# Attention scores of two heads next to each other on TensorE, router constants summed on VectorE

## The chip, the cores and the metric

The kernel runs on one core of a Trainium2 chip. The metric is the device time of one execution in microseconds (us). Three runs of the kernel before took 1401.29, 1407.2 and 1399.86 us; their median is 1401.29.

## What is computed

One inference step of two layers for 512 prompt tokens and 8 decode tokens, which share all weights. Layer 0 mixes tokens with a short gated convolution and with differential attention, layer 1 with mLSTM. Each layer ends with layer norm, a hierarchical mixture of 16 experts, a second layer norm and a gated projection. Cut to what the change touches:

```python
# differential attention, layer 0: 8 heads of 64 (4 pairs), prompt in query blocks of 128
s = einsum('bqhd,bkhd->bhqk', q, k) * 64 ** -0.5
s = where(k_pos[None, :] <= q_pos[:, None], s, -inf)
a = softmax(s).reshape(b, 4, 2, tq, tk)
a = a[:, :, 0] - lam * a[:, :, 1]
o = einsum('bhqk,bkhe->bqhe', a, v)
# router of each layer, after the mixer's layer norm with gain g and offset b
x = (z - mean) * rsqrt(var + eps) * g + b
gl = x @ w_group       # (tokens, 4)
el = x @ w_router      # (tokens, 16)
```

## The kernel before

Five engines work side by side: TensorE (PE) multiplies, VectorE (DVE) and ScalarE (ACT) do the elementwise work, GpSimd (POOL) gathers rows by index, and SyncE's queue (SP) starts most transfers. Each engine takes its instructions in order. The kernel is written in a framework whose planner puts the instructions of each engine into their order when the kernel is built: it goes by the order in which the program traces them and by its own estimates of when each could start. `issue_after` keeps chosen instructions of an engine behind a given one.

**Layer 0's input projection** is one loop (`ws_steps`) over 24 blocks of 128 output columns. Weights come in tiles of 1 MB, two blocks each, from SP's queue. Each block is split into a high part (ACT, L137) and a rest (DVE, L138), 128x1024 elements each, and multiplied in three products of 8 steps over two halves of the tokens: 48 matmuls of 256 or 264 columns at L234, accumulated in one of two PSUM tiles `acc`. The next block is split one step ahead. `consume` functions take a finished block out of PSUM: `rope` for queries and keys (ACT copies to `raw`, PE permutes at L396, DVE at L397 to L399), `vcons` for values, and three for the convolution.

**Between the blocks** stands everything else of the mixer, in generators that the loop steps on (`later`, `advance`), one step per block. Constants are made by five small generators at the steps given by `SM`, each held behind the block's matmuls and split by `behind`: the differential weight, the layer norms' constants `lnT`, the convolution's, the router's (L801) and layer 1's. From step 5 on each step also takes one half page set of a decode sequence's keys: a gather of 1 MB on POOL's queue (L455), a product with the query on DVE (L481) and a sum over each head (L482), 16 times.

**Attention** (`attn`, L502 on) works in 16 units, 4 head pairs by 4 query blocks i, added two at a time from step 11 on; two units stand together on PE and are called a cluster. A unit with query block i has nk = 128(i+1) keys. The two heads of a pair lie on partitions 0 to 63 and 64 to 127 of `qT` and `kT`. For each head PE multiplies 64-row tiles into one PSUM tile `tps` of its own (there are four of these tiles, each one bank), and adds the causal mask to the last 128 columns with a bf16 matmul of the identity with the mask. DVE takes the maximum of each head (L516), ACT the exponential (L519), and DVE joins the heads (L524). A step later PE transposes the result (L266), ACT copies it, PE multiplies with the values (L534).

**Router constants.** The router works on layer norms that have not been scaled yet: with w the router's weights (128 partitions, 8 blocks of the model dimension, 20 columns), g and b the norm's gain and offset, it needs g*w, the sum of b*w over the model dimension, and minus the sum of g*w. Before, the sums are matmuls: for each of the two layers 8 matmuls with b as a column spread over 128 columns (L814), then after g*w is formed (L816), in the generator's next step, 8 matmuls with ones (L821). Each is fp32 and runs as two passes on PE, 64 passes in all. The results are copied from PSUM into `c0` (L815, L822).

**What comes behind.** When the blocks and units are done, the output projection's weights are split and multiplied (`mix_all`), decode attention's values are gathered and summed, and the expert weights of layer 0 are loaded through SP into buffers that come free with the mixer (L155). Then follow routing, experts, projection, and all of layer 1.

Of the kernel before, what the change touches and what calls it, by code (L numbers as in the profile page):

```python
# [8 lines left out]
F32 = mybir.dt.float32  # L9
# [5 lines left out]
OP = mybir.AluOpType  # L15
AX = mybir.AxisListType.X
# [34 lines left out]
SM = (1, 3, 4, 5, 7)  # L51
# [69 lines left out]
class K:  # L121
# [233 lines left out]
    def even(self):  # L355
        tc, nc, A, O = self.tc, self.nc, self.A, self.O
        V, S, G, TE = self.V, self.S, self.G, self.T
# [3 lines left out]
        with tc.tile_pool(name="mz", bufs=1) as mz, tc.tile_pool(name="mx", bufs=1) as mx, tc.tile_pool(name="mx2", bufs=2) as mx2:  # L361
            p, p2 = self.mixer_pools()
# [6 lines left out]
            def lambdas():  # L369
                lv = p2.tile([128, 4, 64], F32, name="lv", tag="e")  # L370
                lp = p2.tile([128, 2, 64], F32, name="lp", tag="e")
                for i, n in enumerate(("lambda_q1", "lambda_k1", "lambda_q2", "lambda_k2")):
                    self.bcast(lv[:, i, :], A[n][0], 64)
                self.bcast(sw, A["subln_w"][0], 128)
                yield
                V.tensor_mul(lp, lv[:, 0::2, :], lv[:, 1::2, :])
                V.tensor_reduce(ls[:, 0:2], lp, axis=AX, op=OP.add)
                S.activation(ls[:, 2:4], ls[:, 0:2], AF.Exp)
                V.tensor_sub(ls[:, 4:5], ls[:, 2:3], ls[:, 3:4])
                V.tensor_scalar(ls[:, 5:6], ls[:, 4:5], 0.2, -1.0, op0=OP.add, op1=OP.mult)  # L380
                V.tensor_scalar_mul(sw, sw, 0.8)
# [122 lines left out]
            def attn(hp, i):  # L504
                nk = (i + 1) * 128
                st = p2.tile([128, 8], F32, name="st", bufs=3)
                e = p2.tile([128, 2, 512], F32, name="e")
                pss = []
                for a in range(2):
                    r = slice(64 * a, 64 * a + 64)  # L510
                    ps = self.tp()
                    pss.append(ps)
                    TE.matmul(ps[:, :nk], qT[r, hp, i * 128:i * 128 + 128], kT[r, hp, :nk], start=True, stop=False)
                    TE.matmul(ps[:, i * 128:nk], self.idb, self.cmb, start=False, stop=True)
                for a in range(2):
                    V.tensor_reduce(st[:, a:a + 1], pss[a][:, :nk], axis=AX, op=OP.max)  # L516
                V.tensor_scalar_mul(st[:, 0:2], st[:, 0:2], -0.125)
                for a in range(2):
                    S.activation(e[:, a, :nk], pss[a][:, :nk], AF.Exp, bias=st[:, a:a + 1], scale=0.125,  # L519
                                 accum_out=st[:, 2 + a:3 + a])  # L520
                V.reciprocal(st[:, 4:6], st[:, 2:4])
                V.tensor_mul(st[:, 5:6], st[:, 5:6], nlam)
                S.mul(e[:, 1, :nk], e[:, 1, :nk], st[:, 5:6])
                V.scalar_tensor_tensor(e[:, 0, :nk], e[:, 0, :nk], st[:, 4:5], e[:, 1, :nk], op0=OP.mult, op1=OP.add)  # L524
                yield
                pt_ = self.tp()
                for j in range(i + 1):
                    self.tr_block(pt_[:, j * 128:(j + 1) * 128], e[:, 0, j * 128:(j + 1) * 128], 128)
                aT = mx2.tile([128, 512], F32, name="aT")
                S.copy(aT[:, :nk], pt_[:, :nk])  # L530
                yield
                po = self.tp()
                for j in range(i + 1):
                    TE.matmul(po[:, :128], aT[:, j * 128:(j + 1) * 128], vt[:, j, hp * 128:(hp + 1) * 128],  # L534
                              start=(j == 0), stop=(j == i))
                o = p2.tile([128, 128], F32, name="o")
                S.copy(o, po[:, :128])
                yield from norm_o(o[:, None, :], 128, 1, hp, slice(i * 128, i * 128 + 128))

                if (hp, i) == (3, 0):  # L540
                    ydone.add(1)

            def norm_o(o, n, nh, hp, cols):

                st = mx2.tile([128, 8], F32, name="st2", bufs=3)
                sq = mx2.tile([128, 128], F32, name="sq", bufs=1)
                for h in range(nh):
                    S.activation(sq[:n], o[:n, h, :], AF.Square, accum_out=st[:n, h:h + 1])
                V.tensor_scalar(st[:n, 0:nh], st[:n, 0:nh], 1.0 / 128, EPS, op0=OP.mult, op1=OP.add)
                G.tensor_tensor(st[:n, 4:4 + nh], st[:n, 0:nh], self.c("nhalf")[:n, 0:nh], op=OP.pow)  # L550
                for h in range(nh):
                    V.scalar_tensor_tensor(o[:n, h, :], o[:n, h, :], st[:n, 4 + h:5 + h], sw[:n], op0=OP.mult, op1=OP.mult)
                yield
                ps = self.tp()
                for h in range(nh):
                    self.tr_block(ps[:, h * n:(h + 1) * n], o[:n, h, :], n)
                S.copy(oT[:, hp:hp + nh, cols], ps[:, :nh * n].rearrange("p (h t) -> p h t", h=nh))
# [6 lines left out]
            def conv_consts():  # L564
                sc = p2.tile([19, 512], F32, name="sc", tag="e")
                nc.sync.dma_start(sc[0:16, :], A["state_conv"][0].rearrange("b j f -> (b j) f"))
                nc.sync.dma_start(sc[16:19, :], A["conv_w"][0])
                yield
                ps = self.tp()
                for f in range(4):  # L570
                    self.tr_block(ps[:, f * 19:(f + 1) * 19], sc[:, f * 128:(f + 1) * 128], 19)
                S.copy(scT, ps[:, :76].rearrange("p (f c) -> p f c", f=4))
                G.memset(uT[:, :, 0:2], 0.0)
# [108 lines left out]
            ydone = set()  # L682
            units = [(hp, i) for i in range(4) for hp in range(4)]

            small = dict(zip(SM, (lambdas(), self.norm_consts(p2), conv_consts(), self.router_consts(), self.odd_consts(p2))))
            s = 0
            soft = None
            while True:
# [26 lines left out]
                if s >= USLOT:  # L715
                    for _ in range(min(2, len(units))):
                        self.later(attn(*units.pop(0)))
# [80 lines left out]
            for i in range(2):  # L798
                self.lnT[n, i] = c[:, z, i].rearrange("p g f -> p (g f)")

    def router_consts(self):  # L801

        V, TE, A, cp = self.V, self.T, self.A, self.cp
        w = cp.tile([128, 2, 8, 20], F32, name="wr")
        c0 = cp.tile([128, 2, 2, 20], F32, name="c0")
        for n, c in (("w_group", slice(0, 4)), ("w_router", slice(4, 20))):
            self.nc.sync.dma_start(w[:, :, :, c], A[n].rearrange("i (k p) c -> p i k c", p=128))
        yield
        for i in range(2):
            gT = self.lnT["ln_mix", i]  # L810
            self.wr[i], self.c0[i] = w[:, i], c0[:, i]
            pc = self.tp()
            for k in range(8):
                TE.matmul(pc[:, 0:20], gT[:, 8 + k:9 + k].to_broadcast([128, 128]), w[:, i, k, :], start=(k == 0), stop=(k == 7))  # L814
            V.tensor_copy(c0[:, i, 0], pc[:, 0:20])  # L815
            V.tensor_tensor(w[:, i], w[:, i], gT[:, 0:8, None].to_broadcast([128, 8, 20]), op=OP.mult)  # L816
        yield
        for i in range(2):
            w, pc = self.wr[i], self.tp()
            for k in range(8):  # L820
                TE.matmul(pc[:, 20:40], self.onf, w[:, k, :], start=(k == 0), stop=(k == 7))  # L821
            V.tensor_scalar_mul(c0[:, i, 1], pc[:, 20:40], -1.0)  # L822

    def mix_load(self, i):

# [1219 lines left out]
```

## Time and profile before

| | |
|---|---|
| median of three runs | 1401.29 us (1399.86 to 1407.2) |
| profiled execution | 1403.28 us, span 1401.5 us |
| PE busy | 1293.0 us (92%), 7944 matmuls |
| DVE busy | 857.8 us (61%), 1500 instructions |
| ACT busy | 628.7 us (45%) |
| POOL busy | 250.8 us (18%) |
| DMA | 338.73 MB, mean 242 GB/s |
| granted PE clock, mean | 0.961 |

The span lies between the first and the last instruction of the profiled execution; the execution's own time stands beside it. Busy time counts an engine's instructions and not its waits. Matmuls overlap each other, so a fully busy PE can still be given less to do. An fp32 matmul appears as two instructions, here called passes. [...]

### The profile page before, as it was taken

Reading aid. Unit: us, or ns where it says so; the run is one execution under the profiler, and the core shown is the slowest. Engines: PE = TensorE matmul, PEld = TensorE weight load, DVE = VectorE, ACT = ScalarE, POOL = GpSimd, SP = SyncE. Lnnn points to the kernel's source line nnn. Section 1 sums busy time; section 2 is a strip of 40 time slices with the busy share of each in tenths; the row PEclk is TensorE's granted clock in tenths of the full one; section 3 lists DMA queues with packets and bytes.
Section 4 is the critical chain, followed back from the end, with each engine's and each line's share of the span. In section 5 each row is a group of like instructions: output and inputs, shape, how many; then the busy total and the mean of one; then the engine's idle time right before and its main releaser. Section 6 shows DMA issues by size and latency. Waiting matters only on the chain. (4 is left out here: it accounts for less than half of the span.)

```text
span 1401.5 us, 21016 instructions
## 1 busy us (share of the span) xinstructions
PE 1293.0 (92%) x7944; PEld 987.0 (70%) x7944; DVE 857.8 (61%) x1500; ACT 628.7 (45%) x1053; POOL 250.8 (18%) x242
## 2 busy tenths in 40 slices
PE   8999998996899999997999999999679999988897
PEld 7998876654676655556989988888457565545686
DVE  4689986546985554435745446774698654544472
ACT  3214465122675544436654333332357554444562
POOL 1023222223211121001130000011312221110113
PEclk9989999997799999999999999999879999999999
DMA  7548644893899999999352223384379999999821
GB/s 271 164 159 296 218 141 156 305 350 124 302 324 373 376 301 353 368 334 312 93 158 70 83 65 125 123 306 181 123 279 327 372 356 315 347 376 344 297 63 39
DMA packets 157449, 338.73 MB, mean 242 GB/s; under 512 B 16095, under 2 KB 54459, under 8 KB 153246
## 3 DMA queue, kind: packets, MB, share of 16 engines
q1 hardware_dynamic: 138974, 271.28, 54.3%
q0 software_dynamic: 18224, 65.98, 15.0%
q8 instruction: 64, 1.05, 0.3%
q14 instruction: 43, 0.35, 0.1%
q10 hardware_dynamic: 144, 0.07, 0.0%
HBM read 313.66 MB, written 32.81 MB: 247 GB/s over the span
## 5 line engine op out<-in xcount | busy, mean ns | idle before, releaser
L138 DVE TENSOR_TENSOR w<-w,sh 128x1024 fp32r<-128x1024 f32 x224 | 267.6, 1221 | 124.4 <-ACT sh L137 104.4
L137 ACT CAST sh<-w 128x1024 fp32r<-128x1024 f32 x224 | 228.0, 1048 | 197.9 <-PE acc L234 108.1
L143 PE MATMUL acc<-w,gh 128*128 128x512 f32 x288 | 119.6, 415 | 7.3 <-DVE w L138 7.3
L142 PE MATMUL acc<-sh,gh 128*128 128x512 f32 x288 | 119.0, 413 | 3.4 <-ACT sh L137 3.4
L144 PE MATMUL acc<-sh,gl 128*128 128x512 f32 x288 | 117.6, 408 | 0.0
L1251 PE MATMUL acc<-w,xT 128*64 128x512 f32 x432 | 109.8, 597 | 3.3 <-DMA w<-in_w_exp_up 3.3
L234 PE MATMUL acc<-x2h,w 128*128 128x256 f32 (+1 forms) x384 | 86.8, 288 | 1.6 <-ACT v L1578 0.8
L234 PE MATMUL acc<-xh,sh 128*128 128x256 f32 (+1 forms) x384 | 85.3, 300 | 2.2 <-ACT sh L137 1.4
L234 PE MATMUL acc<-xh,w 128*128 128x256 f32 (+1 forms) x384 | 81.7, 294 | 0.4 <-DVE w L138 0.4
L234 PE MATMUL acc<-xl,sh 128*128 128x256 f32 (+1 forms) x384 | 81.4, 293 | 0.0
L234 PE MATMUL acc<-x3h,sh 128*128 128x256 f32 (+1 forms) x384 | 80.9, 290 | 0.0
L234 PE MATMUL acc<-x3l,sh 128*128 128x256 f32 (+1 forms) x384 | 78.6, 285 | 0.0
L234 PE MATMUL acc<-x3h,w 128*128 128x256 f32 (+1 forms) x384 | 78.1, 283 | 0.0
L1251 PEld LDWEIGHTS acc<-w,xT 128*64 128x64 f32 x432 | 32.4, 136 | 61.7 <-issue 53.8
L143 PEld LDWEIGHTS acc<-w,gh 128*128 128x128 f32 x288 | 56.3, 196 | 24.3 <-DVE w L138 11.4
L1101 POOL DMA_INDIRECT w<-xd,ix x32 | 47.6, 1488 | 140.2 <-DVE gs L1111 84.0
L142 PEld LDWEIGHTS acc<-sh,gh 128*128 128x128 f32 x288 | 56.5, 196 | 18.7 <-ACT sh L137 5.2
L1312 POOL DMA_INDIRECT ya<-y,ix x18 | 29.3, 1627 | 207.7 <-ACT y L1311 207.7
L234 PEld LDWEIGHTS acc<-x2h,w 128*128 128x128 f32 x384 | 64.5, 189 | 2.5 <-issue 1.3
L234 PEld LDWEIGHTS acc<-xh,sh 128*128 128x128 f32 x384 | 63.6, 198 | 3.6 <-ACT sh L137 1.7
L144 PEld LDWEIGHTS acc<-sh,gl 128*128 128x128 f32 x288 | 56.5, 196 | 13.0
L234 PEld LDWEIGHTS acc<-xh,w 128*128 128x128 f32 x384 | 63.0, 198 | 0.7 <-DVE w L138 0.6
(539 smaller groups left out, 2965.5 us busy)
## 6 DMA issues: line engine op xcount, KB each, us to landing
w<-in_w_exp_gate SPq DMA_DIRECT2D x56, 1024.0 KB, 11.1
w<-in_w_exp_up SPq DMA_DIRECT2D x50, 1024.0 KB, 10.8
w<-in_w_exp_down SPq DMA_DIRECT2D x50, 1024.0 KB, 8.0
wpair<-in_w_exp_up SPq DMA_DIRECT2D x14, 1024.0 KB
w<-in_w_in_even SPq DMA_DIRECT2D x12, 1024.0 KB, 9.7
w<-in_w_in_odd SPq DMA_DIRECT2D x12, 1024.0 KB, 6.0
wpair<-in_w_exp_down SPq DMA_DIRECT2D x10, 1024.0 KB, 13.3
wpair<-in_w_exp_gate SPq DMA_DIRECT2D x8, 1024.0 KB, 7.7
```

Source lines behind the costliest of these rows:

```text
L137: a = self.S.copy(h, src)
L138: self.sp_last = a, self.V.tensor_sub(l, src, h.bitcast(F32))
L142: self.T.matmul(ps, ah, bh, start=start, stop=False)
L143: self.T.matmul(ps, ah, bl, start=False, stop=False)
L144: self.mm3_last = self.T.matmul(ps, al, bh, start=False, stop=stop)
L234: self.mm_last = self.T.matmul(ps[t], a[:, k, :], b[:, k, t0[t]:t1[t]], start=(k == 0 and i == 0), stop=(k == nk - 1 and i == 2))
L1101: self.gather_last = G.indirect_dma_start(out=xg, out_offset=None, in_=rows2(xd) if small else xd, in_offset=bass.IndirectOffsetOnAxis(ap= ...
L1251: TE.matmul(ps[z * HCAP:(z + 1) * HCAP, :], xT[:, a, hf, :], ws[z][:, a, :], start=(hf == 0 and a == 0), stop=(hf == 1 and a == 3))
L1312: G.indirect_dma_start(out=ya, out_offset=bass.IndirectOffsetOnAxis(ap=ix[:, 0:1], axis=0), in_=y, in_offset=None, bounds_check=T - 1, oob ...
```

## The change

In `attn` the mask matmuls move out of the loop over the two heads into a loop of their own: both scores are issued first, then both masks. Operands, PSUM tiles and the rest of the unit stay.

In `router_consts` all sums over the 8 blocks of the model dimension are made on DVE: b*w and g*w for each layer as before or alike, minus g*w, and one reduction over the blocks for both. What is left is a sum over 128 partitions: one matmul with ones for each layer, 40 columns wide, in the generator's last step, and one copy into `c0`. The products lie in a new tile `wrt` with tag "e", which it shares with the exponentials of attention and with small constants (two buffers).

```diff
@@ attn
                     TE.matmul(ps[:, :nk], qT[r, hp, i * 128:i * 128 + 128], kT[r, hp, :nk], start=True, stop=False)
+                for ps in pss:
                     TE.matmul(ps[:, i * 128:nk], self.idb, self.cmb, start=False, stop=True)
@@ even
-self.router_consts()
+self.router_consts(p2)
@@ router_consts
-    def router_consts(self):
+    def router_consts(self, p):
...
         yield
+
+        t = p.tile([128, 3, 8, 20], F32, name="wrt", tag="e")
+        r = t[:, 2].rearrange("p (i z) c -> p i z c", z=4)
         for i in range(2):
             gT = self.lnT["ln_mix", i]
             self.wr[i], self.c0[i] = w[:, i], c0[:, i]
-            pc = self.tp()
-            for k in range(8):
-                TE.matmul(pc[:, 0:20], gT[:, 8 + k:9 + k].to_broadcast([128, 128]), w[:, i, k, :], start=(k == 0), stop=(k == 7))
-            V.tensor_copy(c0[:, i, 0], pc[:, 0:20])
+            V.tensor_tensor(t[:, 0], w[:, i], gT[:, 8:16, None].to_broadcast([128, 8, 20]), op=OP.mult)
             V.tensor_tensor(w[:, i], w[:, i], gT[:, 0:8, None].to_broadcast([128, 8, 20]), op=OP.mult)
+            V.tensor_scalar_mul(t[:, 1], w[:, i], -1.0)
+            V.tensor_reduce(r[:, i, 0:2], t[:, 0:2].rearrange("p z k c -> p z c k"), axis=AX, op=OP.add)
         yield
+        pc = self.tp()[:, 0:80].rearrange("p (i z c) -> p i z c", i=2, z=2)
         for i in range(2):
-            w, pc = self.wr[i], self.tp()
-            for k in range(8):
-                TE.matmul(pc[:, 20:40], self.onf, w[:, k, :], start=(k == 0), stop=(k == 7))
-            V.tensor_scalar_mul(c0[:, i, 1], pc[:, 20:40], -1.0)
+            TE.matmul(pc[:, i], self.onf, r[:, i, 0:2], start=True, stop=True)
+        V.tensor_copy(c0, pc)
```

## Rows read from the trace of the kernel before

**Rows 1.** The page, first part: busy time, share of the span, instructions.
```profile
PE 1293.0 (92%) x7944; PEld 987.0 (70%) x7944; DVE 857.8 (61%) x1500; ACT 628.7 (45%) x1053; POOL 250.8 (18%) x242
```

**Rows 2.** Windows of the mixer: length, busy time of each engine, clock, DMA share.
```profile
94.80:113.70 18.90, 17.61 (x136) 16.07 (x136) 16.92 (x13) 6.32 (x14) 3.48 (x4) 0.99 0.69 239
113.70:145.60 31.90, 31.68 (x226) 28.78 (x227) 29.30 (x48) 13.39 (x44) 9.74 (x9) 0.95 0.84 290
145.60:183.60 38.00, 38.00 (x266) 32.74 (x266) 33.44 (x56) 21.76 (x66) 11.55 (x13) 0.96 0.59 204
183.60:226.90 43.30, 42.10 (x273) 31.93 (x273) 32.41 (x76) 25.88 (x80) 8.03 (x11) 1.00 0.37 130
```

**Rows 3.** PE's waits, 0 to 245 us: in total, times, longest.
```profile
PE tps L266 <- DVE e L524: 1.0, 2, 0.6
...
PE acc L234 <- DVE w L138: 0.4, 1, 0.4
```

**Rows 4.** SP's timeline behind the mixer: start, length, instruction, count.
```profile
234.15 4.06 SPq L155 DMA_DIRECT2D w<-in_w_exp_gate  x2
```

**Rows 5.** PE's timeline: scores (L513) at i=0, then at i=3.
```profile
110.33 0.49 PE L513 MATMUL tps<-kT,qT 64*128 64x128 f32 x2 [0.88 <-ACT vt L411]
...
110.90 0.48 PE L513 MATMUL tps<-kT,qT 64*128 64x128 f32 x2
...
209.47 1.12 PE L513 MATMUL tps<-kT,qT 64*128 64x512 f32 x2
...
210.68 1.12 PE L513 MATMUL tps<-kT,qT 64*128 64x512 f32 x2
```

**Rows 6.** PE's timeline: expert matmuls on two column halves, alternating.
```profile
412.99 3.65 PE L1251 MATMUL acc<-w,xT 128*64 128x512 f32 x16
```

**Rows 7.** PE's timeline: both groups of the router's constants and the rotary matmul behind.
```profile
68.92 3.65 PE L814 MATMUL tps<-wr,lnT 128*128 128x20 f32 x32
...
79.80 4.13 PE L821 MATMUL tps<-wr,onf 128*128 128x20 f32 x32
83.77 2.08 PE L396 MATMUL tps<-raw,cst 128*128 128x256 f32 x4
```

**Rows 8.** Windows of L234 alone, one weight block each: PE, weight loads, clock, DMA.
```profile
62.16:68.05 5.89, 5.89 (x48) 5.84 (x48) 1.00 0.73 236
72.41:79.80 7.39, 7.39 (x48) 7.34 (x48) 0.77 0.89 316
85.27:93.19 7.92, 7.92 (x48) 7.77 (x48) 0.73 0.49 139
```

**Rows 9.** DVE's groups by form, 60 to 235 us: busy us, mean ns, idle before.
```profile
L516 DVE TENSOR_REDUCE st<-tps 128x1 f32<-128x384 f32 x8 | 4.3, 551 | 2.1 <-PE tps L514 2.1
...
L816 DVE TENSOR_TENSOR wr<-wr,lnT 128x160 f32<-128x160 f32 x2 | 0.6, 316 | 0.0
...
L815 DVE COPY c<-tps 128x20 f32<-128x20 f32 x2 | 0.3, 171 | 0.0
```

**Rows 10.** DVE's timeline: first key product, then the splits behind it.
```profile
64.03 2.28 DVE L481 TENSOR_TENSOR w<-w,qb 128x2048 f32<-128x2048 f32 x1
...
91.85 1.21 DVE L138 TENSOR_TENSOR w<-w,sh 128x1024 fp32r<-128x1024 f32 x1
...
112.44 2.35 DVE L138 TENSOR_TENSOR w<-w,sh 128x1024 fp32r<-128x1024 f32 x2
```

**Rows 11.** DVE's waits, 60 to 235 us: in total, times, longest.
```profile
DVE rtmp L397 <- PE tps L396: 6.0, 4, 3.9
DVE st L516 <- PE tps L514: 5.5, 13, 0.9
...
DVE c L822 <- PE tps L821: 3.4, 1, 3.4
```

**Rows 12.** Windows of two half-clock stretches, columns as in rows 2.
```profile
113.50:116.90 3.40, 3.19 (x14) 3.20 (x15) 3.40 (x8) 0.81 (x4) 1.01 (x1) 0.50 0.95 349
171.54:174.90 3.36, 3.36 (x14) 2.39 (x13) 2.49 (x4) 1.24 (x4) 0.29 (x1) 0.50 0.70 224
```

More of the change, by code (lines that the diff above doesn't have):

```diff
@@ L683, in even @@
             units = [(hp, i) for i in range(4) for hp in range(4)]
-            small = dict(zip(SM, (lambdas(), self.norm_consts(p2), conv_consts(), self.router_consts(), self.odd_consts(p2))))
+            small = dict(zip(SM, (lambdas(), self.norm_consts(p2), conv_consts(), self.router_consts(p2), self.odd_consts(p2))))
             s = 0
```

## The prediction

> **What bounds the kernel now.** The page comes first: TensorE (PE) is busy for 92% of the span [rows 1]. That is an average over stages, so the second view is the table of windows over the stage that the diff touches, the even layer's mixer from 95 to 227 us [rows 2]. The reader is to see two full columns there: PE is never under 93% of a window, and VectorE (DVE) fills 16.9 of 18.9, 29.3 of 31.9 and 33.4 of 38.0 us up to 183.6, and lets go only behind that (32.4 of 43.3). The third view, PE's waits, says how close the two are: PE has waited for DVE's split of a weight block only once, for 0.4 us [rows 3], but that wait falls where DVE's splits come out at 112.4, straight before the matmuls that need them. So up to about 184 us a microsecond taken from PE is worth something only as far as DVE also comes forward. Behind 184 us PE alone sets the pace, with short waits for the attention chain (1.0 us in two, same group). What comes after the mixer starts when the mixer lets it: the first expert weights are issued at 234.15 us, behind the mixer's last blocks [rows 4]. A gain at 227 us therefore moves everything behind it, and I carry it to the end one for one.
>
> **Scores and masks.** There are 16 units (4 head pairs by 4 query blocks i), each with two heads' scores, each score an fp32 matmul that the chip runs as two passes, and one bf16 mask. Score and mask of one head take 0.57 us at i=0 (110.33 to 110.90) and 1.21 at i=3 (209.47 to 210.68) [rows 5]. The difference, 0.64 over 384 columns, is two passes of 0.107 us per 128 columns; at 512 columns a pass streams 0.427. What is left of the 0.57, 0.36 us, doesn't depend on the width: the mask itself and its two changes between a 64-row and a 128-row array.
> After the change the two scores stand next to each other, on rows 0 to 63 and 64 to 127, and write two PSUM tiles; then come both masks. [...] No row of this kernel shows two row groups. The nearest shows two column groups: 16 fp32 passes of 512 columns in 3.65 us [rows 6], where one behind the other would be 16 x 0.427 = 6.8; that is eight pairs side by side, of 0.43 to 0.46 each. By this row the second score costs nothing: two passes a unit, 0.213 x (1+2+3+4) x 4 = 8.5 us. Bounds: 0 (row groups don't overlap) and 8.5; I take 8.5, from the nearest row. The edit takes 13.4 us off PE, at most. Over the eight clusters of two units that is 1.04 each at i=0, 1.46 at i=1, 1.89 at i=2, 2.32 at i=3.
> [...]
>
> **Router constants.** Now two groups of 32 passes with 20 columns: 3.65 and 4.13 us, with what follows them 3.5 and 4.0 us later [rows 7]. [...] Without them I expect the clock to stay: 1.5 + 2.0 back. The two matmuls that remain are four passes of 40 columns, about 0.5 us by the 0.114 of a 20-column pass. PE: 7.5 + 3.5 - 0.5 = 10.5 us less.
> DVE gets more to do. Gone are four small PSUM copies of 0.17. New are, twice, one multiplication like L816's (0.32), a negation of 160 elements (taken as 0.25: between a small copy's 0.17 and 0.32) and a reduction of 320 elements (0.5, next to the 0.55 of a 384-element reduction) [rows 9], and one copy: 2.3 - 0.7 = 1.6 us more. Bounds: 0.6 (all at the small-copy price) and 3 (issue gaps). The new tile takes a turn of the buffers with tag "e", long before attention needs them; nothing waits there.
> The gain on PE meets DVE's queue here. DVE starts the decode keys' multiplications at 64.03 (2.28 us, a reduction as long behind each) and only gets to the split of the next missing block at 91.85, to the two after it at 112.44 [rows 10]. This queue is in order and nothing of the change shortens its work, so blocks of PE that use these splits come forward only by DVE's own idle time. That is 3.4 us for the router's matmul and 6.0 - 3.9 = 2.1 for the rotary matmul queued behind it (the 3.9 lies before 64 us) [rows 11]: 5.5 us. Less the 1.6 of new work: **3.9 us** arrive at 113.7, of PE's 10.5 and the first cluster's 1.0. Bounds: 1.5 (1.6 us hidden nowhere and the waits half kept) and 8 (the planner pulls the splits ahead of the key products).
>
> **From 113.7 us on.** PE gives 1.04 + 2 x 1.46 + 1.89 = 5.9 us up to 184. DVE must follow. It waits 5.5 us for masks in 13 places [rows 11], about 3 of it before 184, and the rest of its idle time belongs to the softmax chain. I count **4.0** of the 5.9. Behind 184 PE gives 1.89 + 2 x 2.32 = 6.5; the softmax of the last pair (ACT and DVE in turn, PE waits for it already) keeps some 2: **4.5**. Bounds for both together: 3 (DVE and the chain keep most) and 13. Where the cover is lost: PE waits longer for splits and chain, which costs nothing beyond what is already taken off.
> **Sum:** 3.9 + 4.0 + 4.5 = 12.4 us. The profiled execution took 1403.3 us (span 1401.5), the median of the runs is 1401.3. Off the median: 1401.3 - 12.4 = 1388.9, so **1389 us**.
>
> **Rivals.**
> *Passes in order.* The second head's first pass runs beside the first head's second: three pass times instead of two, so 4.3 us less than 13.4: 9.1, of which 8.3 past the first cluster. At the same yield (8.5 of 12.4) the attention part is 5.7: 1401.3 - 3.9 - 5.7 = 1391.7. [...] Against: the interleaved column pair. With no overlap at all, 4.3 x 0.69 = 3.0: 1394.4.
> *VectorE is the bound.* DVE yields nothing beyond the router's waits, the softmax chain takes all but 2 us of the late gain: 1401.3 - 3.9 - 2 = 1395.4. For it: DVE at 88 to 92% up to 183.6. Against: its waits for masks shrink by themselves.
> *The clock turns it.* Slower than before. The half-clock stretches at 113.5 and 171.5 us each stand behind a cluster of scores [rows 12], in which only half of the array's rows work and PE idles or switches. If the shorter clusters, with new waits for DVE in front of the blocks at 95 and 113 us, are each followed by a half-clock stretch, then six clusters more pay 1.5 and the two waits 2.0: 13 us against a gain of 12.4, 1402 us. It decides from eight extra stretches on. Against: six of eight clusters now have none, and side by side both halves of the array work.
> *Another order.* The planner orders each engine's work by its own estimates, and on its account PE also gets shorter. If it puts the splits in front of the key products, PE's full 24 us come within reach less DVE's slack: some 20 us, 1381. A worse order costs as much; no row bears on the sign.
>
> **Chances.** Forecast 0.48 (own range 1384 to 1394), passes in order or no overlap 0.16, VectorE 0.18, the clock or a worse order 0.11, a better order 0.07. What a measurement can tell from no change is 0.5%, 7 us: below 1394.3 or above 1408.3. Faster: 0.48 x 0.9 + 0.16 x 0.8 + 0.18 x 0.2 + 0.07 = 0.66; slower: under half of the 0.11, 0.06; the rest 0.28. Range: 1380 (a better order, or both upper bounds in part) to 1399 (VectorE with the lower bounds).
>
> **What would show it.** Score pairs: at i=3 both scores begin within 0.1 us or at least the second's first pass before the first's second, and a unit takes 1.3 us instead of 2.43; at 1.7 passes run in order, at 2.1 not at all. Router: no 20-column group, granted clock 1.00 where it now falls behind both groups, each block of 48 passes there at 5.9. DVE: the split of 91.85 comes at about 88, that of 112.4 at about 108.5; PE waits several us for the splits in between, and "DVE w L138" rises from 0.4 to the head of its waits. The first expert weights are issued at about 222 instead of 234. I am wrong if the mixer ends as much earlier and the end does not (a later stage is bound by something of its own), or if the splits come out in another order.

## The result, and the profile after

The changed kernel took 1394.21 us (median of ten runs, 1385.67 to 1400.73), the kernel before 1400.03 us in ten runs beside it: ratio 0.995, 95% interval 0.9931 to 0.9969. Two later measurements of the same kernel gave 1390.97 (ratio 0.9943, 0.9921 to 0.9965) and 1390.79 us (0.9943, 0.9926 to 0.9959). It is faster by half a per cent; 1389 was forecast. The profiled execution took 1390.96 us (before 1403.28); that the spans of these two differ by just the 12.4 us of the forecast is chance, since the medians differ by 5.8.

The page's line of busy times, which answers to [rows 1]: PE has 25.1 us less to do, the span is 12.4 us shorter, DVE's busy time is the same.

```profile
PE 1267.9 (91%) x7884; PEld 967.1 (70%) x7884; DVE 858.5 (62%) x1503; ACT 627.9 (45%) x1053; POOL 254.0 (18%) x242
```

PE's timeline at a unit of i=3 (start, length, line, count), the answer to [rows 5]: four passes in one group, and the next unit begins 1.28 us behind the first, where it was 2 x 1.21. In the single records behind this row the second head's first pass starts 7 ns after the first head's (194.933 and 194.940), and the second passes 6 ns apart (195.467 and 195.473). In one of the 16 units, at 144.97 us (i=1), the heads' passes still stand one behind the other, there and in every other kernel with the new scores but e10; why isn't known.

```profile
194.93 1.13 PE L513 MATMUL tps<-kT,qT 64*128 64x512 f32 x4
196.00 0.28 PE L515 MATMUL tps<-cmb,idb 128*128 128x128 bf16 x2
196.21 1.13 PE L513 MATMUL tps<-kT,qT 64*128 64x512 f32 x4
```

PE's timeline where the router's constants were, for [rows 7]: 0.53 us in place of 3.65 and 4.13, then the rotary matmul, and then a wait of 2.11 us that was not there before.

```profile
72.92 0.53 PE L823 MATMUL tps<-wrt,onf 128*128 128x40 f32 x4
73.28 1.12 PE L396 MATMUL tps<-raw,cst 128*128 128x256 f32 x4
76.52 0.51 PE L234 MATMUL acc<-xh,sh 128*128 128x256 f32 x2 [2.11 <-ACT raw L391]
```

The weight blocks around it, windows of L234 alone as in [rows 8] (start:end, length, PE busy, weight loads, granted clock with 1.00 as full speed, DMA share, GB/s). The block at 66.97, which was the one at 72.41 before, now keeps the full clock. The block at 76.52, which was the one at 85.27, stands behind the new wait and still runs into a half-clock stretch. The one at 85.52 comes after it.

```profile
60.40:66.30 5.90, 5.90 (x48) 5.84 (x48) 1.00 0.69 233
66.97:72.92 5.95, 5.95 (x48) 5.87 (x48) 1.00 0.30 72
76.52:83.93 7.41, 7.41 (x48) 7.36 (x48) 0.77 0.88 287
85.52:91.40 5.88, 5.88 (x48) 5.83 (x48) 1.00 0.70 243
```

DVE's timeline: the new work of the router's first layer (four instructions, then the same again from 57.45), the first key product, and the splits that answer to [rows 10]. The new work stands in front of a rotary step that waits for PE anyway (0.53 us, where DVE waited 3.9 us before); the splits come at 84.39 and 105.28 instead of 91.85 and 112.44. Ahead of the second one DVE now waits 2.44 us for a load of queries, `qb`.

```profile
55.68 0.32 DVE L816 TENSOR_TENSOR wrt<-wr,lnT 128x160 f32<-128x160 f32 x1
56.03 0.32 DVE L817 TENSOR_TENSOR wr<-wr,lnT 128x160 f32<-128x160 f32 x1
56.39 0.24 DVE L818 TENSOR_SCALAR wrt<-wr 128x160 f32<-128x160 f32 x1
56.67 0.75 DVE L819 TENSOR_REDUCE wrt<-wrt 128x40 f32<-128x320 f32 x1
...
59.71 0.42 DVE L397 TENSOR_TENSOR rtmp<-tps,cs 128x256 f32<-128x256 f32 x1 [0.53 <-PE tps L396]
...
62.27 2.28 DVE L481 TENSOR_TENSOR w<-w,qb 128x2048 f32<-128x2048 f32 x1
...
84.39 1.21 DVE L138 TENSOR_TENSOR w<-w,sh 128x1024 fp32r<-128x1024 f32 x1
...
98.68 2.29 DVE L481 TENSOR_TENSOR w<-w,qb 128x2048 f32<-128x2048 f32 x1 [2.44 <-DMA qb<-qd]
...
105.28 2.35 DVE L138 TENSOR_TENSOR w<-w,sh 128x1024 fp32r<-128x1024 f32 x2
```

The mixer's second part in windows, for [rows 2]. The 69.9 us from 113.7 to 183.6 are now the 62.8 from 106.5 to 169.3, and DVE is busy for 61.47 of them, 98%, where it was 90%; the last 43.3 are 41.5, and in them PE is busy for 37.30 where it was 42.10.

```profile
106.50:169.30 62.80, 61.70 (x492) 56.69 (x494) 61.47 (x102) 34.87 (x109) 22.42 (x22) 1.00 0.76 260
169.30:210.84 41.54, 37.30 (x275) 30.14 (x275) 32.28 (x77) 25.79 (x81) 6.69 (x11) 1.00 0.43 153
```

PE's waits up to 229 us, for [rows 3], hold the new ones that the account below rests on. L520 is ACT's exponential, L553 DVE's scaling of the attention output; of the 2.9 us for L520, 2.3 lie behind 169 us.

```profile
PE tps L266 <- ACT e L520: 2.9, 4, 1.1
...
PE acc L234 <- ACT raw L391: 2.1, 1, 2.1
PE tps L266 <- DMA colr<-in_mh_norm_w: 2.0, 1, 2.0
...
PE tps L266 <- DVE o L553: 1.3, 2, 0.8
PE acc L234 <- DVE w L138: 0.7, 1, 0.7
```

The first expert weights are issued at 218.09 (SP's timeline, for [rows 4]).

```profile
218.09 4.07 SPq L155 DMA_DIRECT2D w<-in_w_exp_gate  x2
```

So the mixer ends 16.06 us earlier, of which 1.76 are an earlier start of the whole execution: 14.3. Behind layer 0 the offset stays, until between 3 and 4 us are lost in one place, where layer 1's gates are multiplied (L1663, L1661 before). There the waits of all engines, 706.6 to 718 us (in total, times, longest), show the stores of the activations (`x3d`, L1597) and the copies in front of them (`st`, L1591) held up one behind the other; the window table gives a half-clock stretch behind them.

```profile
POOL x3d L1597 <- ACT st L1591: 5.5, 2, 3.3
...
PE tps L266 <- ACT st L1591: 4.1, 2, 2.4
ACT st L1591 <- DMA x3d<-st: 3.5, 2, 1.8
```

```profile
706.60:711.60 5.00, 3.24 (x26) 2.07 (x24) 3.27 (x8) 3.00 (x9) 2.52 (x4) 1.00 0.38 122
711.60:715.10 3.50, 1.15 (x11) 0.67 (x9) 1.34 (x6) 1.40 (x4) 0.39 (x1) 1.00 0.02 2
715.10:718.60 3.50, 3.50 (x19) 2.09 (x18) 0.00 (x0) 0.00 (x0) 1.02 (x4) 0.52 0.14 39
```

What stands out in this stretch is one packet of a queue that belongs to no line of the program and that the page calls `instruction`: 16 KB at 711.5 us that took 1.34 us, called an instruction fetch here. The page counts such fetches in one line, 64 in the whole execution, against 15,768 matmuls and weight loads on PE: one for 246 of these. That they are PE's is borne out by e5 and e6 below, where PE instructions alone move the one next to the gates from 4.9 us behind them to 4.9 ahead, and from 4.8 ahead to 4.6 behind. The 16 completions of the store waited for came in from 711.94 to 713.95; in the kernel before, where the nearest fetches start at 718.36 and 734.94, from 728.09 to 728.27.

```profile
q8 instruction: 64, 1.05, 0.3%
```

The last of the 16 completions came 2.01 us behind the first where a fetch was under way and 0.18 us behind it where none was.

### The profile page after: what moved, and what is told of

It reads as the page before. It is cut to its first block, busy times and chain, and to the rows that moved or that the text cites. A ratio compares the mean times of both kernels' runs of the same rounds, so it can differ in the third digit from the quotient of the medians.

```text
span 1389.1 us, 20899 instructions
## 1 busy us (share of the span) xinstructions
PE 1267.9 (91%) x7884; PEld 967.1 (70%) x7884; DVE 858.5 (62%) x1503; ACT 627.9 (45%) x1053; POOL 254.0 (18%) x242
## 5 line engine op out<-in xcount | busy, mean ns | idle before, releaser
L138 DVE TENSOR_TENSOR w<-w,sh 128x1024 fp32r<-128x1024 f32 x224 | 267.4, 1221 | 123.1 <-ACT sh L137 104.3
L234 PE MATMUL acc<-x2h,w 128*128 128x256 f32 (+1 forms) x384 | 86.9, 288 | 1.6 <-ACT v L1580 0.7
L234 PE MATMUL acc<-xh,sh 128*128 128x256 f32 (+1 forms) x384 | 83.2, 294 | 5.4 <-ACT sh L137 2.2
L234 PE MATMUL acc<-x3h,sh 128*128 128x256 f32 (+1 forms) x384 | 80.9, 290 | 0.0
L234 PE MATMUL acc<-xl,sh 128*128 128x256 f32 (+1 forms) x384 | 79.9, 287 | 0.0
L234 PE MATMUL acc<-xh,w 128*128 128x256 f32 (+1 forms) x384 | 79.2, 287 | 0.7 <-DVE w L138 0.7
L234 PE MATMUL acc<-x3l,sh 128*128 128x256 f32 (+1 forms) x384 | 78.6, 285 | 0.0
L234 PE MATMUL acc<-x3h,w 128*128 128x256 f32 (+1 forms) x384 | 78.1, 283 | 0.0
L143 PEld LDWEIGHTS acc<-w,gh 128*128 128x128 f32 x288 | 55.9, 194 | 24.9 <-DVE w L138 12.4
L234 PEld LDWEIGHTS acc<-xh,sh 128*128 128x128 f32 x384 | 61.5, 192 | 7.2 <-ACT raw L391 2.5
L234 PEld LDWEIGHTS acc<-x2h,w 128*128 128x128 f32 x384 | 64.5, 189 | 2.4 <-issue 1.3
L143 PE MATMUL acc<-w,hh 128*128 128x512 f32 x144 | 60.2, 418 | 2.1 <-DVE w L138 2.0
```

The lines of the kernel that those rows point to most:

```text
L138: self.sp_last = a, self.V.tensor_sub(l, src, h.bitcast(F32))
L143: self.T.matmul(ps, ah, bl, start=False, stop=False)
L234: self.mm_last = self.T.matmul(ps[t], a[:, k, :], b[:, k, t0[t]:t1[t]], start=(k == 0 and i == 0), stop=(k == nk - 1 and i == 2))
```

## The experiments

All profiles in one table. A is the time from the first rotary matmul (L396) to the first score (L513), B from there to the first matmul of the decode values (L669, L668 before), C from layer 1's gates to the end of the span; in brackets the time at half clock within A and B. F is where, counted from the gates, the instruction fetch nearest to them starts. Ratios are to the kernel before, beside it.

| kernel | ratio (95%) | A, us | B, us | C, us | F, us |
|---|---|---|---|---|---|
| before | | 76.8 (10.2) | 126.4 (6.8) | 678.4 | -4.8 |
| before again (e1) | 1.0006 (0.9989 to 1.0024) | 75.7 (6.8) | 123.5 (0) | 678.4 | -4.9 |
| after | 0.9950 (0.9931 to 0.9969) | 72.1 (6.8) | 116.8 (0) | 682.5 | +4.9 |
| after again (e2) | 0.9943 (0.9921 to 0.9965) | 71.6 (0) | 120.1 (6.8) | 683.8 | +5.0 |
| after, third (e11) | 0.9943 (0.9926 to 0.9959) | 72.3 (6.8) | 116.9 (0) | 682.5 | +4.6 |
| scores only (e3) | 0.9973 (0.9954 to 0.9991) | 75.4 (6.8) | 117.5 (0) | 677.7 | -4.8 |
| router only (e4) | 0.9992 (0.9977 to 1.0006) | 71.9 (0) | 124.5 (3.4) | 681.9 | +4.5 |
| after, fetches moved (e5) | 0.9914 (0.9892 to 0.9936) | 70.2 (3.4) | 120.2 (6.8) | 678.8 | -4.9 |
| the same again (e12) | 0.9931 (0.9909 to 0.9954) | 71.7 (6.8) | 117.1 (0) | 677.3 | -4.8 |
| scores only, fetches moved (e6) | 0.9970 (0.9948 to 0.9991) | 77.0 (10.2) | 119.8 (6.8) | 682.2 | +4.6 |
| before, short key sums (e7) | 1.0009 (0.9996 to 1.0021) | 78.8 (6.8) | 122.6 (6.8) | 678.3 | -4.9 |
| router only, short key sums (e8) | 0.9947 (0.9928 to 0.9966) | 74.3 (3.4) | 120.2 (6.8) | 678.9 | +3.8 |
| after, short key sums (e10) | 0.9915 (0.9887 to 0.9942) | 74.6 (3.4) | 110.7 (3.4) | 678.9 | +3.7 |
| after, fetches moved, norm row early (e9) | 0.9894 (0.9873 to 0.9914) | 67.6 (0) | 117.8 (0) | 678.5 | -4.7 |

Two things are read from it at once. B differs between executions of one kernel by its half-clock time: with half of that taken off, the three with the old scores and full key sums give 123.0, 123.5 and 122.8, the seven with the new ones 116.4 to 117.5 (e9, with another change in it, 117.8). And A of the changed kernel is 71.6 to 72.3 in its three profiles, whether it holds 0 or 6.8 us of half clock; there the clock of PE doesn't count, so PE does not set the pace.

**Both kernels once more, and each part alone (e1 to e4).** No edit in e1 and e2. e3 is the kernel before with the masks' loop alone, e4 the kernel after without it:

```diff
 # e3: before, and e4 the other way round
+                for ps in pss:
                     TE.matmul(ps[:, i * 128:nk], self.idb, self.cmb, start=False, stop=True)
```

> The kernel before, a second time, for another profiled execution and more times. Theory A (the mixer's 14 us are the same in every execution and are carried to the end; the two profiled executions differ by 12.4 while the medians differ by 5.8 because the rest of the program varies by several us from run to run): decode attention's first value product (L668), at 236.7 us in the first profile, starts at 234.5 to 237.5 again, counted from the start of the rotary loop within 1 us of the first profile, and what varies lies behind 240 us. Theory B (the first profile of before had a slow mixer): L668 starts 4 us or more earlier, at 229 to 233.

> The changed kernel a second time. Theory A: the first value product (L669) starts at 220 to 223 us as in the first profile (220.7), and the ratio to before tends to 0.990 to 0.995 with more runs. Theory B (the first profile of the changed kernel had a fast mixer): at 224 us or later. Theory C (what the mixer gains is given back behind it in most executions): L669 at 220 to 223, but the stretch from there to the end is longer than the 1164.8 us of before by 4 us or more, at one place that both profiles of the changed kernel show (the first shows 3.5 us lost in layer 1's input at about 712 us).

> Scores of two heads next to each other, router constants as before. By the prediction's terms 4.0 + 4.5 us arrive: L669 at 228 us. By what the profile of both shows (half-clock stretches behind clusters gone, 7.1 + 1.8 behind 113.7 us): about 9 us, L669 at 227 to 228, granted clock 1.00 from 116 us on. Rival (VectorE is the bound and the clusters' gain needs the router's head start): 4 us or less, 232. Time against before: -8 us by the first, -3 by the rival.

> Router constants on VectorE, scores as before. By the prediction: VectorE's split that waited until 112.4 us comes 3.9 us earlier; by the first profile of both 5.4, because the new work falls into an idle stretch of VectorE at 56 us. L668 then starts 4 to 6 us earlier, at 231 to 233. Rival (TensorE sets the pace): the 10.5 us that TensorE has less to do arrive, L668 at 226. Time against before: -5 us; by the rival -10.

Of the expectations, e1's theory B came true: L668 starts at 232.3 us. e2 shows two of its theories at once: L669 starts at 224.7 (B), and the stretch from there to the end is 1169.0 us, 4.2 longer than before, at the place that the first profile had shown (C). e3 has L669 at 226.9 as expected, but its time is 3.8 us less, near the rival's 3 and not 8. e4 has L668 at 230.8, at the edge of what was expected, and 1.1 us less instead of 5.

The first profile of before had a slow mixer: A and B together are 203.2 us there and 199.1 in e1, and it holds 10.2 us more at half clock, half of which is enough for the difference. The scores alone shorten B by 5.6 us with the clock taken out (117.5 against 123.1, the mean of the three old ones) and leave A alone. The router alone shortens A by 4.3 (71.9 against 76.2, the mean of before, e1, e3 and e6) and leaves B. The parts add up in the mixer. At the end they don't: C is 3.5 to 5.4 us longer than in before in every one of these kernels that has the new router, and the router alone measures as no change.

**The fetches moved (e5, e12, e6).** The new router has 60 passes less, with their weight loads 120 instructions, about half of the 246 that stand to one fetch; so every later fetch falls on other work. e5 and e12 (the same kernel) put 120 instructions back, in the first 5 us, where PE waits for its first input (4.3 us in the profile after). e6 does it to the kernel with the scores alone: 136 instructions more and 120 fewer differ by 256, about one whole fetch.

```diff
 # e5, e12: after; e6: scores only, with range(68)
+            pad = self.tp()
+            for _ in range(60):
+                self.T.matmul(pad[:, 0:1], self.onb, self.onb[:, 0:1], start=True, stop=True)
```

> The changed kernel with 60 one-column bf16 matmuls (120 instructions with their weight loads) ahead of everything, in the first 5 us, where TensorE waits for its first input. [...] Theory (the router change gives 3 to 4 us back at layer 1's gates because a fetch now lands on the stores that the gates wait for): no lag of those stores, gates to end 678 us as before instead of 682 to 684, time 3 to 4 us under the changed kernel's: ratio to the kernel before 0.991 to 0.992. Rival (the loss comes from something else of the router change): gates to end stays at 682 to 684, ratio 0.994 to 0.995.

> [...] Theory: the lag of the stores appears at layer 1's gates without any change of the router: gates to end 681 to 682 us instead of 678, ratio 0.999 to 1.000 instead of the 0.9973 of scores alone. Rival: gates to end stays at 678, ratio 0.997.

> The changed kernel with the 60 one-column matmuls ahead once more, now beside the changed kernel on the same chip: the ratio of the first time, 0.9914, overlaps the 0.9943 of the changed kernel. Theory: gates to end 678 to 679 us and 3 to 4 us less time than the changed kernel. Rival: within 1 us of it, the fetch's cost being given back elsewhere.

C went back to 678.8 and 677.3 in the changed kernel, and up to 682.2 in the kernel whose router is the old one. Over all fourteen profiles C is 681.9 to 683.8 in the five whose fetch starts 4.5 to 5.0 us behind the gates, and 677.3 to 678.9 in the nine where it starts elsewhere, router changed or not. In the traces it is thus shown both ways that the loss follows the fetch. The waits of e12 in the same stretch as above, 707.2 to 719 us (line numbers are three higher there):

```profile
POOL x3d L1600 <- ACT st L1594: 3.8, 2, 2.3
...
PE tps L266 <- ACT st L1594: 1.8, 2, 1.3
...
ACT st L1594 <- DMA x3d<-st: 1.3, 1, 1.3
```

```profile
712.20:715.70 3.50, 2.93 (x25) 2.03 (x24) 1.05 (x5) 1.00 (x3) 1.27 (x2) 1.00 0.15 40
715.70:719.20 3.50, 3.50 (x31) 3.10 (x29) 1.02 (x7) 2.49 (x4) 0.14 (x2) 1.00 0.03 5
```

The wait for the store is 1.3 us instead of 3.5, PE waits 1.8 instead of 4.1, and the clock stays. The 4 us are thus 2.3 of waiting and half of a stretch of 3.4 us at half clock. In time the loss isn't shown: by the ratios it is 1.7 us (e12 beside e11, 0.9931 against 0.9943), 4.1 (e5, 0.9914 against 0.9943 of e2) and -0.4 (e6, 0.9970 against 0.9973 of e3), each uncertain by some 4 us. e6's ratio is its rival's number and not the 0.999 to 1.000 that I expected; its runs lie between 1386.95 and 1404.46 us, so only its trace speaks for the theory.

The records of all fourteen profiles say more on the fetch. Where it starts 4.5 to 5.0 us behind the gates, the 16 completions of the store at 3.3 to 3.8 us are spread over 1.65 to 2.01 us, the last comes 1.0 to 1.1 us behind the end of the fetch, and the gates end 12.0 to 12.8 us behind their start. Where it starts at 3.7 or 3.8 us (e8, e10), the spread is 1.09 and 0.90 us and the gates end at 10.2 and 9.9, so such a fetch costs some 0.8 us and not nothing; no half-clock stretch follows there. In the other seven the spread is 0.15 to 0.19 us and the gates end at 9.1 to 9.4. It was not shown that the fetch and the last completion share one DMA engine. The 60 matmuls also take one turn of the four PSUM tiles `tps`, and the new router takes three turns fewer; but e9 below takes as many as the changed kernel and has a C of 678.5, so which tile falls where doesn't make the loss.

**VectorE relieved (e7, e8, e10).** The key sums take 4 of 64 elements of each head (most of the sums is left out), 2.28 us down to 0.28 for each of 16 reductions, in the kernel before, in the one with the router alone, and in the changed one:

```diff
-                                w.rearrange("p t (h d) -> p t h d", h=8), axis=AX, op=OP.add)
+                                w.rearrange("p t (h d) -> p t h d", h=8)[:, :, :, 0:4], axis=AX, op=OP.add)
```

> The kernel before with VectorE's key-sum reductions of the decode rows over 4 of 64 elements of each head (most of the sums is left out), some 30 us less work on VectorE ahead of 113 us. Theory (VectorE bounds the mixer up to 113.7 us, so that of the router's 10.5 us only about 5 arrive): TensorE takes over the bound, the mixer becomes some 3 to 6 us shorter than the 199 to 203 us of the kernel before. Rival (TensorE sets the pace already): the mixer is unchanged within 2 us. It is also the base for the run with the router change on top.

> The same short key sums with the router change alone. Theory (VectorE bounds the mixer): with its load gone the router change is worth its full 9 to 10.5 us in the mixer, against the same kernel without it, where it was worth 3 to 7 with the full load. Rival: it stays at about 5 us. The difference of the two times may hold 3 to 4 us less than that of the two mixers, by the fetch at layer 1's gates.

> The changed kernel with the key sums over 4 of 64 elements of each head (most of the sums is left out). Base: the same sums without the change, mixer 201.4 us (rope to decode values), 1401.2 us; with the router change alone 194.5 and 1395.0. Theory (VectorE keeps part of both gains): with its load gone the attention edit gives 9 to 13 on top of the router's 6.9, mixer 182 to 186 us, against 189 to 192 in the changed kernel with full sums. Rival (VectorE keeps only the router's part; the attention edit yields the 8.3 us of scores alone): mixer 186 to 188. Rival 2 (nothing is kept by VectorE): 189 to 192.

In the kernel before the relief is worth nothing (1.0009). The window from 33 to 113 us shows why, of before, of e7 and of e8 in turn (PE is the first engine, DVE the third):

```profile
33.00:113.00 80.00, 78.56 (x583) 74.94 (x581) 57.33 (x64) 19.39 (x31) 9.83 (x8) 0.94 0.57 180
```

```profile
33.00:113.00 80.00, 79.97 (x613) 77.05 (x612) 52.50 (x72) 20.95 (x33) 13.91 (x10) 0.96 0.65 214
```

```profile
33.00:113.00 80.00, 76.22 (x588) 73.11 (x587) 58.80 (x83) 21.72 (x37) 18.80 (x11) 0.98 0.72 243
```

PE was full already, so the theory that VectorE bounds the kernel before is wrong as I put it for e7: TensorE paced it, with VectorE close behind. But the router change is worth 0.0062 of the time with the relief (0.9947 against 1.0009, 8.7 us) and 0.0008 without it (1.1 us, or about 5 without the loss at the gates). By the times VectorE then holds back some 4 us as soon as PE has less to do, a difference that the intervals of these ratios don't clear. In the mixer 6.9 us arrive with the relief (201.4 to 194.5), under the 9 to 10.5 of the theory and over the 5 of the rival. What PE still waits for in e8 up to 112 us is one thing, 3.8 us for a load of 4 KB, about what is missing:

```profile
PE tps L266 <- DMA colr<-in_mh_norm_w: 3.8, 1, 3.8
```

With the scores too (e10) A and B together are 185.3, in the range of the theory (182 to 186). B falls from e8 to e10 by 7.8 us, clock taken out (116.8 to 109.0), from e4 to the seven new ones (mean 116.9) by 5.9: about 2 us of the attention's gain are kept where the key sums are whole. They are late ones: from the second cluster of i=2 to the decode values e10 takes 57.8 us and e8 63.1, while with whole sums it is 51.5 against 53.3. In e10 PE doesn't wait for the exponential there.

**The norm row early (e9).** That load, layer 1's norm weights, takes its turn in the two buffers of the tag "qb" with the queries of the key products. In the changed kernel SP waits for it before the next queries may be loaded (SP's waits, 60 to 112 us), and DVE waits 2.44 us for these queries, as shown above.

```profile
SPq L134 <- DMA colr<-in_mh_norm_w: 5.9, 1, 5.9
```

e9 is e5 with the row loaded and transposed together with the other norms:

```diff
-        r = p.tile([64, 128], F32, name="colr", tag="qb")
+        r = p.tile([72, 128], F32, name="colr", tag="qb")
...
+        self.nc.sync.dma_start(r[64:72, :], A["mh_norm_w"][0].rearrange("(f p) -> f p", p=128))
...
-        wg, nwr = p.tile([128, 8, 8], F32, name="colr", tag="qb"), p.tile([8, 128], F32, name="colr", tag="qb")
+        wg = p.tile([128, 8, 8], F32, name="colr", tag="qb")
```

> The changed kernel with the 60 one-column matmuls ahead, and with layer 1's norm weights (4 KB) loaded and transposed together with the other norm weights early, so that TensorE has no matmul at 93 us that waits for a load of its own (it waited 2.0 us in the changed kernel, 0.9 with the 60 matmuls, 3.8 with the router change and short key sums). Theory (VectorE's queue sets 60 to 113 us): the waits move to the splits, less than 1 us comes forward at the first scores; time as with the 60 matmuls alone, 0 to 2 us less. Rival (that load sets the pace there): the first scores come 2 us earlier and the end too.

I expected under 1 us in A. It fell to 67.6, by 2.6 to 4.1 us against e5 and e12, on the rival's side. The reason is not that PE set the pace: DVE does, and the load had been holding up DVE too. In e9's timeline the two key products stand without a gap, and the windows behind 75 us show DVE busy from end to end:

```profile
94.08 4.48 DVE L484 TENSOR_TENSOR w<-w,qb 128x2048 f32<-128x2048 f32 x2
98.48 4.46 DVE L485 TENSOR_REDUCE sall<-w 128x32 f32<-128x2048 f32 x2
102.86 2.34 DVE L138 TENSOR_TENSOR w<-w,sh 128x1024 fp32r<-128x1024 f32 x2
```

```profile
75.00:95.00 20.00, 16.47 (x129) 15.25 (x128) 20.00 (x20) 5.70 (x11) 5.88 (x4) 1.00 0.70 244
95.00:113.00 18.00, 16.38 (x136) 15.48 (x135) 18.00 (x21) 6.65 (x18) 9.86 (x5) 1.00 0.85 301
```

With 1385.5 us, 0.9894 (0.9873 to 0.9914), e9 beats both kernels; beside it the changed kernel measured 0.9943 (0.9926 to 0.9959). Against the fetches alone, e12 beside it with 0.9931 (0.9909 to 0.9954), the intervals touch. From the decode values to the gates e9 took 491.6 us, where the others took 484.1 to 489.2; what it gives back there was not followed.

> The changed kernel as it is, on the same chip as the three others, as their base. Expected: ratio 0.994 to 0.995 to the kernel before; gates to end 682 to 684 us, with the instruction fetch 4.4 to 4.9 us behind the gates and a half-clock stretch behind it.

e11, with no edit, came out as expected.

## Why the prediction was right, and where not

**What bounds the kernel.** Right up to 184 us: PE paces, DVE is close behind, and what is taken from PE counts as far as DVE follows. e7 showed the first half (relief of DVE alone is worth nothing); that DVE then paces is shown by A in the changed kernel, which doesn't follow the clock, and by e9. Wrong behind 184 us, as told below: PE alone doesn't set the pace there.

**Scores.** Right: 1.28 us a unit where 1.3 was forecast, and neither rival of the overlap (1.7, 2.1) holds. The records show both first passes and then both second ones, two pass times in all (in 15 of 16 units). What fails is the order that the first rival assumed, the second head's first pass beside the first head's second, by which a unit would have taken 1.7 us; no record shows the order of issue. In the prediction's 13.4 us 4.9 stand for the two masks one behind the other, 0.31 a unit, by a price of a mask alone that no run shows. In the profile after the two masks of a unit start 0.065 to 0.067 us apart, and a unit of i=3 takes 1.15 us less than the 2.43 of before, 0.85 for two passes and 0.30 for the rest.

**Router, on PE.** Right in the passes (7.5 - 0.5) and in the block behind the first group (5.95 at full clock, so in all nine kernels with the new router). The 3.5 in PE's 10.5 is what the two later blocks of [rows 8] take beyond the 5.89 of the first, 1.5 and 2.0; that both clocks fell because of the 20-column passes was an assumption. The block behind the second group took 7.41 us at 0.77 in this profile, so of the 2.0 put back for it 0.5 came. Not foreseen: with the passes gone PE comes early to that block, whose PSUM tile ACT has not emptied yet, and waits 2.11 us. Of the seven profiles with this wait four have a half-clock stretch in the block behind it and three (e2, e4, e9) have none, so the wait alone doesn't decide it; and A of e2 and e4 is hardly shorter for it (71.6 and 71.9).

**Router, on DVE.** The new work (L816, L818 and L819 twice, and the copy of 0.23) is 2.8 us where 2.3 had been put: the reduction takes 0.74 and not 0.5. It cost nothing all the same, since it stands in what was DVE's longest wait. The splits come 52.6 us behind the first rotary matmul in all six kernels with the new router and full key sums, and 57.4 to 58.8 in the four with the old one; the second pair at 72.3 to 73.9 instead of 77.5 to 78.9 (e9 left aside). That is some 5, the 5.5 us of idle time of [rows 11], and not 3.9. That DVE takes its queue in order, as the account of its idle time assumes, shows in the profile before: the key sum L482 had its product at 78.28 and started at 81.79, behind a copy (L822) that waited 3.42 us for PE.

```profile
76.00 2.28 DVE L481 TENSOR_TENSOR w<-w,qb 128x2048 f32<-128x2048 f32 x1
81.70 0.18 DVE L822 TENSOR_SCALAR c<-tps 128x20 f32<-128x20 f32 x1 [3.42 <-PE tps L821]
81.79 2.28 DVE L482 TENSOR_REDUCE sall<-w 128x32 f32<-128x2048 f32 x1
```

"PE waits several us for the splits" is wrong: DVE w L138 holds it only 0.7 us; the wait for ACT and the one for the norm row, 2.1 and 2.0, take the rest. Both stand behind VectorE's queue in turn: ACT's copy waits 1.9 us for DVE's kT L399, and the norm row's load stands in SP's queue behind two others that wait for DVE, 11.7 us for a key product (L481) and 4.9 us for a split (wgl L138). A itself falls by 4.6 us (76.2 to 71.6, the mean of the six with the new router and full key sums, e9 left aside) where 3.9 was forecast. With half of their half-clock time taken off, the four with the old router take 71.7 to 72.3, nearly what the new ones take: by this account what arrived in A is what the slow clock had cost, and the passes themselves hardly count, since DVE's queue needs these 71.6 us.

**From there on.** Forecast 4.0 + 4.5, measured 6.2 in B, 123.1 to 116.9 (by the windows of the first pair of profiles 7.1 and 1.8, with 6.8 us of half clock in before and none after). The first term was right: from the first score to the second cluster of i=2 it is 69.8 us in the three with the old scores and 65.4 in the seven with the new ones, clock taken out: 4.4 less, with DVE 98% busy in the profile after. The second term failed: "Behind 184 us PE alone sets the pace", with some 2 us kept by the softmax. From that cluster to the decode values it is 53.3 us in the three and 51.5 in all seven, with no half clock in any: 1.8 instead of 4.5. PE is busy for 5.1 us less there (51.7 to 46.6) and waits longer for the chain of ACT and DVE, 4.4 us (2.3 of it for the exponential L520 and 1.3 for L553, as shown above) instead of 1.0. The mixer as a whole gave 10.8 of 12.4.

**To the end.** By the traces this step failed as well: "A gain at 227 us therefore moves everything behind it, and I carry it to the end one for one." The way it fails had been named as what would prove me wrong, but with no mechanism and no price: 4 us are given back 480 us later, by an edit that doesn't touch that place. The sum closes so: 1400.0 (the base measured beside it, 1.3 under the median used) less 10.8, plus 4.1, is 1393.3; without the 4.1 it is 1389.2. Measured were 1394.2, 1391.0 and 1390.8, between the two or just above, so the times alone don't tell how much of the 4.1 counts in most executions.

**Rivals.** "VectorE is the bound" was half right: its 2 us for the late gain is what came (1.8), its nothing for the stretch up to 184 us is not (4.4). "The clock turns it" fell: A and B hold 6.8 us of half clock after and 6.8 to 17.0 before. "Another order" fell up to 184 us: DVE's splits and key products stand in the same order, but for the router's work. From there on DVE's and ACT's orders in the mixer do change with the new scores (not in e4), and what that does to the late 1.8 us was not separated. Behind the mixer PE's order is the same.

## What to carry to other kernels

Up to 113 us PE was 98% busy here (78.56 of 80.00 us), and of the 10.5 us that the router's change was to take from it 4.6 arrived in A, within what DVE's queue had in idle time, 5.5 us [rows 11]; before summing, read the idle time of the next engine's queue, and look at which buffers its instructions free. Where PE waits for a softmax chain even a little, here 1.0 us, price what is taken from PE by that chain: of 5.1 us 1.8 arrived. Here 120 PE instructions fewer also moved the later instruction fetches, and in the traces one fell on a store that the next stage waits for, at a cost of about 4 us: when an edit costs time far behind its place, compare the fetches with the stores there, and move them by some instructions in idle time. Between single profiles of one kernel, take half of the half-clock time off a stretch that TensorE paces before comparing; what is left of B agrees within about 1 us here (122.8 to 123.5, and 116.4 to 117.5).

## What was not expected of the hardware

Two fp32 matmuls on the two halves of the array's rows ran side by side in 15 of 16 units, and fully so at 512 columns: 1.13 us for both where one took 1.12 [rows 5]. A fetch of 16 KB of instructions took 0.88 to 1.43 us in 121 of 128 cases in the profiles of before and after, and up to 1.88 in the others; in the traces it cost about 4 us when it started 4.5 to 5.0 us behind the gates of layer 1, some 0.8 at 3.7 or 3.8, and nothing to be seen elsewhere. Half-clock stretches fell at places that change from one execution to the next: 0 to 17 us of them within A and B in the fourteen profiles.
